# Expert weights in pieces of 16 KB per partition, and the second-last expert's scatter in four PSUM banks

## The chip, the cores and the metric

The kernel runs on one core of one Trainium2 chip. The metric is the device time of one execution in microseconds (us), as the median of three runs. All tensors are fp32.

## What is computed

One layer over 256 latent tokens of width 1024, with 256 context tokens ahead of them. Two mixers (a bidirectional state-space scan and a gated DeltaNet) read the same normalised input; their gated sum goes through an output projection `w_out`. Then comes a mixture of 32 experts, 4 of them per token, and a last RMSNorm. The part that fills most of the time is the mixture:

```python
for e in range(N_EXPERTS):                       # 32
    gu = t @ w_gate_up[e] + b_gate_up[e]         # 1024 -> 2048
    gate, up = gu[:, :D_EXPERT], gu[:, D_EXPERT:]
    gate = jnp.minimum(gate, 7.0); up = jnp.clip(up, -7.0, 7.0)
    act = (up + 1.0) * gate * jax.nn.sigmoid(gate * 1.702)
    out = out + combine[:, e:e + 1] * (act @ w_down[e] + b_down[e])
```

An expert has 8 MB of `w_gate_up` and 4 MB of `w_down`; all 32 have 384 MB (402.7 million bytes), and each byte is read once from HBM.

## The kernel before

**Front** (to about 500 us): modulation, input projection, the two mixers, the branch projections, `merge` (L1307: gates times branches, `w_out`, residual, second norm) and the router. Its large intermediates live in 15 registers of 8 KB per partition (`r`, tags such as XC, R2, H0, PA) and five load buffers (`ld`).

**Experts.** `moe` (L1435) takes one expert after the other. For each, `gather` (L1567) picks up to 64 of its tokens with one-hot matmuls and transposes them to `xT`; `Expert.gu` multiplies by gate-up, one *unit* of 1 MB (128 rows of 2048) after the other, 8 units; `swiglu` (L1686) makes `ut` on VectorE and ScalarE; `down` (L1702) transposes `ut` on PE (`ident,ut`) to `aT` and takes the 4 units of `w_down`; `weigh` (L1721) makes `od` on VectorE, its rounded part `odh` on ScalarE and the rest `odl`; `scatter` (L1733) multiplies these with the one-hot `ST` into PSUM banks and VectorE adds them to `x1` (`x<-x,ps`). A unit is 8 matmuls in the profile, 4 in the order of the program.

**The weights' stream.** 12 units per expert are read in the order in which PE wants them: four gate-up units of the next expert, four of w_down, the other four gate-up units. `wtile` (L1405) takes the places of a ring in turn, `wload` (L1412) issues the load from SP:

```python
WREG = ("K", "XL", "XC", "R2", "U", "H0", "H1", "V", "Q", "R3", "GA") + ("ld",) * 5 + ("PA", "s1", "PB")
NPRE = 10
```

That is 19 places of 1 MB. 18 of them take a unit by one DMA with 8 KB in one piece per partition, "s1" by two DMAs with 4 KB pieces. In `merge` the first load is issued, then the four loads of `w_out` (`wo`), then ten more units; the rest as places come free. SP executes its instructions in the order of the program, so one that waits for a place holds back all behind it. The other engines' order is made by a scheduler from the program. The last expert takes its w_down units in the order 0, 2, 1, 3, and `swiglu` and `down` in two parts.

Of the kernel before, what the change touches and what calls it, by code (L numbers as in the profile page):

```python
# [7 lines left out]
F32 = mybir.dt.float32  # L8
# [8 lines left out]
D = 1024  # L17
EPS = 1e-6
NH = 4
NE = 32  # L20
# [3 lines left out]
def dram(ap, off, dims):  # L24
    return bass.AP(tensor=ap.tensor, offset=ap.offset + off, ap=dims)


class Kern:
# [3 lines left out]
    def build(self):  # L32
        with ExitStack() as es:
            tc = self.tc
            self.con = es.enter_context(tc.tile_pool(name="con", bufs=1))
            self.dr = es.enter_context(tc.tile_pool(name="dr", bufs=1, space=DRAM))
            self.ps = es.enter_context(tc.tile_pool(name="ps", bufs=2, space=PSUM))
            self.consts()
            self.wk = es.enter_context(tc.tile_pool(name="wk", bufs=1))
            with tc.manual_schedule(engines={mybir.EngineType.SP}):  # L40
                self.front()
                self.moe()
# [6 lines left out]
    def w(self, shape, name, tag=None, dt=F32):  # L49
# [7 lines left out]
        assert n <= size, (name, n)  # L57
        return self.wk.tile(list(shape), dt, name=name, tag=tag, bufs=bufs)

    def r(self, reg, name, dt=F32):  # L60

        assert reg in self.REGS
        return self.wk.tile([128, 2048], dt, name=name, tag="r" + reg, bufs=1)

    LD = 5

    def ld(self, name, dt=F32):

# [1311 lines left out]
        self.tt(self.lc, self.lc, p[:, :NE], OP.add)  # L1380


    WREG = ("K", "XL", "XC", "R2", "U", "H0", "H1", "V", "Q", "R3", "GA") + ("ld",) * 5 + ("PA", "s1", "PB")
    NPRE = 10
    HPOOL = [3]
    WOUT = [[0, [0, 1, 2, 3, 4, 5, 6, 7]], [1, [0, 1, 2, 3, 4, 5, 6, 7]]]
    BBP = 0
# [2 lines left out]
    DOWN, DOWN_LAST = (0, 1, 2, 3), (0, 2, 1, 3)  # L1390

    def moe_stream(self):
        I = self.I
        self.nw, self.wq = 0, []
        gu = lambda e, j: dram(I["w_gate_up"], (e * D + j * 128) * 2048, [[2048, 128], [1, 2048]])

        dn = lambda e, f: dram(I["w_down"], (e * D + 512 * (f // 2) + 2 * (f % 2)) * D, [[4 * D, 128], [1, 2 * D]])
        src = [gu(0, j) for j in range(8)]
        n = self.AHEAD
        for e in range(NE):  # L1400
            a = [gu(e + 1, j) for j in range(8)] if e + 1 < NE else []
            src += a[:n] + [dn(e, f) for f in (self.DOWN if a else self.DOWN_LAST)] + a[n:]
        self.wsrc = iter(src)

    def wtile(self):  # L1405
        rg = self.WREG[self.nw % len(self.WREG)]
        self.nw += 1
        if rg == "s1":
            return [self.w([128, D], "w", rg) for _ in range(2)]
        return [self.ld("w") if rg == "ld" else self.r(rg, "w")]  # L1410

    def wload(self, src):  # L1412

        w = self.wtile()
        if len(w) == 1:
            if self.nw == 12 * NE:
                for f in range(2):
                    self.nc.sync.dma_start(w[0][:, f * D:f * D + D], src[:, f * D:f * D + D])
            else:
                self.nc.sync.dma_start(w[0] if len(src.shape) == 2 else w[0].rearrange("p (f c) -> p f c", f=2), src)  # L1420
            return lambda i: w[0][:, 512 * i:512 * i + 512]
        for h in range(2):
            self.nc.sync.dma_start(w[h], src[:, 1024 * h:1024 * h + 1024] if len(src.shape) == 2 else src[:, h])
        return lambda i: w[i // 2][:, 512 * (i % 2):512 * (i % 2) + 512]

    def moe_load(self):
        self.wq.append(self.wload(next(self.wsrc)))

    def moe_weights(self):
        if not self.wq:  # L1430
# [4 lines left out]
    def moe(self):  # L1435
        tc, nc, I = self.tc, self.nc, self.I
# [72 lines left out]
        def expert(e):  # L1509

            keep = None
            if e == NE - 1:
                left = (12 * NE - 1 - self.WREG.index("GA")) % len(self.WREG)
                while self.nw < 12 * NE - left:
                    self.moe_load()
                keep = self.r("GA", "keep")
                self.nf = self.r("R3", "nf")
# [12 lines left out]
        for e in range(NE - 1):  # L1530
            cur.gu(6)
            nxt = expert(e + 1)
            cur.gu(8)
            cur.swiglu()
            nxt.gu(self.AHEAD)
            cur.down(self.DOWN)
            if e == NE - 2:

                cur.weigh()
                nxt.gu(8)  # L1540
                with tc.issue_after(self.last.ins):
                    nxt.swiglu(2)
                    cur.scatter()
            else:
                nxt.gu(self.AHEAD + 1)
                cur.weigh()
                cur.scatter()
            cur = nxt
# [17 lines left out]

    def gather(self, x, pos, cw, io64, keep=None, first=False):  # L1567

        nc = self.nc
        oh = self.w([128, 2, 2, CAP], "oh", "c2")  # L1570
        for t in range(2):
            self.nc.vector.tensor_scalar(oh[:, t], io64[:, None, :].to_broadcast([128, 2, CAP]), pos(t), None,
                                         op0=OP.is_equal)
        xT = self.w([128, 8, CAP], "xT", "p5")
        if first:

            x.xT = xT
            for js in self.FIRST:
                p = self.pt("o").rearrange("p (j s) -> p j s", s=CAP)
                for j in js:  # L1580
                    for t in range(2):
                        self.mm(p[:, j], self.h2[:, t, 128 * j:128 * j + 128], oh[:, t, 0], start=(t == 0), stop=(t == 1))
                x.gu(js[0])
                self.act(xT[:, js[0]:js[-1] + 1], p[:, js[0]:js[-1] + 1], AF.Copy)
        else:

            p = self.pt("o")
            for t in range(2):
                for dh in range(2):
                    self.mm(p[64 * dh:64 * dh + 64], oh[:, t, 0], self.h2[:, t, 512 * dh:512 * dh + 512],  # L1590
                            start=(t == 0), stop=(t == 1))
            xg = self.w([128, 512], "xg", "g5")
            self.act(xg, p, AF.Copy)
            p = self.pt("o")
            for q in range(4):
                self.tr(p[:, 128 * q:128 * q + 128], xg[:, 128 * q:128 * q + 128], self.ident)
            self.act(xT.rearrange("p (d q) s -> p q d s", d=2), p.rearrange("p (q d s) -> p q d s", q=4, d=2), AF.Copy)
        p = self.pt("o")
        for t in range(2):
            o2 = oh[:, t].rearrange("p d s -> p (d s)")  # L1600
            self.tr(p[:, 128 * t:128 * t + 128], o2, self.ident)
# [12 lines left out]
    def overflow(self, pos, cmb, cnt, io64):  # L1614
# [1 line left out]
        tc, nc, I = self.tc, self.nc, self.I  # L1616
        V = nc.vector
        assert not self.wq
        self.WREG = [r for r in self.WREG if r not in ("GA", "R3")]
# [7 lines left out]
        with tc.If(most > CAP):  # L1627
# [10 lines left out]
            with tc.For_i(0, NE, 1) as e:  # L1638
# [3 lines left out]
                for b in range(1, 256 // CAP):  # L1642
                    with tc.If(ce > CAP * b):
# [7 lines left out]
                        wg = I["w_gate_up"][0, bass.ds(e, 1)].rearrange("o (j p) f -> (o p) j f", p=128)  # L1651
                        wd = I["w_down"][0, bass.ds(e, 1)].rearrange("o (h p r) d -> (o p) h r d", p=128, r=4)
                        x = Expert(self, lambda j: self.wload(wg[:, j]), lambda f: self.wload(wd[:, f // 2, 2 * (f % 2):2 * (f % 2) + 2]),
                                   lambda i: (row[:, 128 * i:128 * i + 128], brow), (row[:2, :128], drow))
                        self.gather(x, lambda t: pe[:, t:t + 1], lambda t: pe[:, 2 + t:3 + t], io64)
                        x.gu(8)
# [6 lines left out]
class Expert:  # L1663
# [66 lines left out]
        k.act(oh, od, AF.Copy)  # L1730
        k.tt(ol, od, oh.bitcast(F32), OP.subtract)

    def scatter(self):  # L1733
        k = self.k
        for t in (1, 0):
            ps = [k.pt("s"), k.pt("s")]
            for o in self.od:
                for dh, r in enumerate(self.HALF):
                    k.mm(ps[dh], self.ST[r, 128 * t:128 * t + 128], o[r], start=(o is self.od[0]), stop=(o is self.od[-1]))
# [49 lines left out]
```

## Time and profile before

| | us |
|---|---|
| median of three runs (1449.15, 1453.27, 1454.15) | 1453.27 |
| the profiled execution's own time | 1453.78 |
| its span | 1452.1 |
| PE (TensorE matmuls) busy | 1338.0 (92%) |
| DVE (VectorE) busy | 559.1 (39%) |
| ACT (ScalarE) busy | 255.4 (18%) |
| POOL (GpSimd) busy | 179.1 (12%) |
| DMA traffic of the core | 473.06 MB, mean 326 GB/s |

Busy time is that of one execution; PE's ends are modelled, so a busy PE isn't PE at its peak. PEld is PE's load of the stationary operand, which overlaps its matmuls. A bracket such as [1.57 <-ACT odh L97] says how long the engine stood idle ahead of an instruction and what ended it.

### The profile page before, as it was taken

To read this page: it belongs to the slowest core of one execution; us is meant where nothing else is said; L and a number is where in the kernel's file an instruction comes from. 1 tells how busy PE (TensorE), PEld (TensorE's weight loads), DVE (VectorE), ACT (ScalarE), POOL (GpSimd) and SP (SyncE) were. 2 spreads that over 40 slices of the span, in tenths; PEclk is the share of its full clock that TensorE was granted. 3 is DMA by queue.
4 is the path that set the end of the run, shared out by engine and by line. 5 is a ranking of instruction groups with operands and counts; after the bars stand their busy time and mean duration, and the time that the engine had idled before them with its cause. 6 is when DMAs were issued, how large, how long until landed. Compare 5 with 4: busy or idle time off the path is not lost. (4 is left out here: it accounts for less than half of the span.)

```text
span 1452.1 us, 18531 instructions
## 1 busy us (share of the span) xinstructions
PE 1338.0 (92%) x7469; PEld 600.9 (41%) x7469; DVE 559.1 (39%) x1083; ACT 255.4 (18%) x568; POOL 179.1 (12%) x299
## 2 busy tenths in 40 slices
PE   4799784999999899999999999999999999999985
PEld 1244362768787533333333333333333333333321
DVE  4977977664254403222322322232222222222213
ACT  3224321524301111011110110111011101111001
POOL 1921875111000100000000000000000000000000
PEclk9799896999999899999999999999999999999998
DMA  9464236711638899999999999999999999999994
GB/s 341 193 139 146 88 77 178 223 59 59 197 123 329 281 356 416 419 419 420 419 418 419 420 418 419 419 420 418 419 420 419 418 420 419 419 419 419 419 420 188
DMA packets 93275, 473.06 MB, mean 326 GB/s; under 512 B 24912, under 2 KB 29160, under 8 KB 41344
## 3 DMA queue, kind: packets, MB, share of 16 engines
q1 hardware_dynamic: 73216, 461.08, 79.4%
q10 hardware_dynamic: 19968, 10.73, 3.5%
q8 instruction: 61, 1.00, 0.3%
q14 instruction: 30, 0.25, 0.1%
HBM read 466.52 MB, written 3.16 MB: 323 GB/s over the span
## 5 line engine op out<-in xcount | busy, mean ns | idle before, releaser
L79 PE MATMUL ps<-w,xT 128*64 128x512 f32 x2048 | 485.7, 601 | 9.0 <-DMA w<-in_w_gate_up_dram 8.8
L79 PEld LDWEIGHTS ps<-w,xT 128*64 128x64 f32 x2048 | 137.6, 137 | 272.6 <-issue 241.8
L79 PE MATMUL ps<-w,aT 128*64 128x512 f32 x1024 | 233.1, 597 | 11.4 <-DMA w<-in_w_down_dram 11.1
L1725 DVE SCALAR_TENSOR_TENSOR od<-ps,cs,gt 128x512 f32<-128x512 f32 x31 | 23.3, 750 | 468.7 <-PE ps L79 468.7
L79 PEld LDWEIGHTS ps<-w,aT 128*64 128x64 f32 x1024 | 71.6, 137 | 165.5 <-issue 126.4
L94 DVE TENSOR_TENSOR x<-x,ps 128x512 f32<-128x512 f32 x128 | 84.1, 684 | 66.4 <-PE ps L79 66.4
L1506 POOL CAST selsd<-biad 128x128 fp32r<-128x128 f32 x32 | 9.4, 294 | 703.5 <-PE ps L79 703.5
L97 ACT ACTIVATE odh<-od 128x512 fp32r<-128x512 f32 x31 | 19.5, 629 | 427.0 <-DVE od L1725 427.0
L79 PE MATMUL ps<-h,win 128*128 128x512 f32 x192 | 91.3, 616 | 0.0
L79 PE MATMUL ps<-hx,wsp 128*128 128x256 f32 (+1 forms) x384 | 81.8, 360 | 0.0
L79 PEld LDWEIGHTS ps<-hx,wsp 128*128 128x128 f32 x384 | 62.9, 198 | 20.1 <-issue 9.8
L79 PE MATMUL ps<-h,oh 128*64 128x512 f32 x248 | 63.0, 604 | 0.0
L79 PEld LDWEIGHTS ps<-h,win 128*128 128x128 f32 x192 | 35.0, 195 | 47.6 <-issue 45.8
L97 ACT ACTIVATE sgm<-gt 128x512 f32<-128x512 f32 (+1 forms) x33 | 20.3, 618 | 163.6 <-DVE gt L1696 163.6
L79 PE MATMUL ps<-wm,sc 128*32 128x512 f32 x192 | 29.3, 699 | 20.2 <-DMA wm<-in_w_mod_dram 20.2
L97 ACT ACTIVATE aT<-ps 128x512 f32<-128x512 f32 (+1 forms) x33 | 19.3, 584 | 141.9 <-PE ps L83 141.9
L1696 DVE TENSOR_SCALAR gt<-ps 128x512 f32<-128x512 f32 (+1 forms) x33 | 22.2, 675 | 57.1 <-PE ps L79 57.1
L94 DVE TENSOR_TENSOR wsp<-win,wsp 128x512 fp32r<-128x512 f32 x48 | 32.0, 701 | 23.8 <-ACT wsp L97 23.5
L685 DVE SCALAR_TENSOR_TENSOR cacc<-raw,col_gdn_conv,cacc 128x512 f32<-128x512 f32 (+1 forms) x48 | 36.3, 756 | 5.5 <-ACT cacc L97 5.3
L1506 POOL CAST selsg<-biad 128x256 fp32r<-128x256 f32 x32 | 13.7, 427 | 190.7 <-PE ps L79 184.5
L97 ACT ACTIVATE wsp<-win 128x512 fp32r<-128x512 f32 x48 | 27.5, 624 | 49.2 <-PE ps L79 27.0
L79 PE MATMUL ps<-bias,selsg 128*128 128x512 f32 x64 | 28.6, 472 | 7.1 <-DVE ut L1698 6.6
(367 smaller groups left out, 1465.9 us busy)
## 6 DMA issues: line engine op xcount, KB each, us to landing
w<-in_w_gate_up_dram SPq DMA_DIRECT2D x242, 1024.0 KB
w<-in_w_down_dram SPq DMA_DIRECT2D x121, 1024.0 KB
wm<-in_w_mod_dram SPq DMA_DIRECT2D x24, 1024.0 KB
win<-in_w_in_dram SPq DMA_DIRECT2D x18, 1024.0 KB
w<-in_w_gate_up_dram SPq DMA_DIRECT2D x28, 512.0 KB
w<-in_w_down_dram SPq DMA_DIRECT2D x14, 512.0 KB
wo<-in_w_out_dram SPq DMA_DIRECT2D x4, 1024.0 KB
wa<-in_w_branch_a_dram SPq DMA_DIRECT2D x4, 512.0 KB
```

The source lines that it names most:

```text
L79: self.last = self.nc.tensor.matmul(out, lhsT, rhs, start=start, stop=stop, **kw)
L94: (eng or self.nc.vector).tensor_tensor(out, a, b, op=op)
L97: self.nc.scalar.activation(out, in_, func, **kw)
L685: nc.vector.scalar_tensor_tensor(acc[:, rows], rt[:, rows, k:k + 64], sc, acc[:, rows], op0=OP.mult, op1=OP.add)
L1506: nc.gpsimd.tensor_copy(v.rearrange("p (n s) -> p n s", s=CAP), dup[:, x:x + n, None].to_broadcast([128, n, CAP]))
L1696: V.tensor_scalar(g, z0, 7.0, None, op0=OP.min)
L1725: V.scalar_tensor_tensor(od, self.pd, self.cs, k.gt2, op0=OP.mult, op1=OP.mult)
```

## The change

Twelve registers are joined to six pairs of 16 KB per partition (`PAIRS`: pa = XC and R2, pb = XL and U, pc = H0 and H1, pd = V and Q, pe = R3 and GA, pf = PA and PB), and the front uses their halves. The ring now has nine places of 2 MB. Six are the pairs: each takes two units by one DMA of 2 MB, 16 KB in one piece per partition (gate-up rows 256 j + 2 p and the next; w_down's rows 4 p to 4 p + 3 of one half). The other three are made of "ld" buffers and K and take two DMAs of 8 KB pieces. "s1" is in the ring no more, so it holds 18 MB. The first place of the ring is pa. The last two places of the stream (the last expert's w_down) are loaded in 8 KB pieces, and the very last unit in two halves. Since gate-up rows stand in other partitions, `gather` reads every second column for `xT`. `keep` and the final norm's gain share the tile pe. The second-last expert's `scatter` takes the four PSUM banks s, o, p, g, where it took two of s in turn.

```diff
+    PAIRS = dict(pa=("XC", "R2"), pb=("XL", "U"), pc=("H0", "H1"), pd=("V", "Q"), pe=("R3", "GA"), pf=("PA", "PB"))
+    def both(self, tag, name):
+        return self.wk.tile([128, 4096], F32, name=name, tag=tag, bufs=1)
+    def part(self, tag, half, dt):
+        if tag not in self.pairs:
+            self.pairs[tag] = self.both(tag, "t" + tag)
+        v = self.pairs[tag][:, 2048 * half:2048 * half + 2048]
+        return v if dt is F32 else v.bitcast(dt)
...
-    WREG = ("K", "XL", "XC", "R2", "U", "H0", "H1", "V", "Q", "R3", "GA") + ("ld",) * 5 + ("PA", "s1", "PB")
-    NPRE = 10
+    WREG = ("pa", "pb", "pc", "pe", "pd", "ld", "ld", "k", "pf")
+    NPRE = 4
...
-        gu = lambda e, j: dram(I["w_gate_up"], (e * D + j * 128) * 2048, [[2048, 128], [1, 2048]])
-        dn = lambda e, f: dram(I["w_down"], (e * D + 512 * (f // 2) + 2 * (f % 2)) * D, [[4 * D, 128], [1, 2 * D]])
+        gu = lambda e, j: dram(I["w_gate_up"], (e * D + 256 * j) * 2048, [[4096, 128], [1, 4096]])
+        dn = lambda e, h: dram(I["w_down"], (e * D + 512 * h) * D, [[4 * D, 128], [1, 4 * D]])
...
+        l = dn(NE - 1, 0), dn(NE - 1, 1)
+        src[-2:] = [tuple(x[:, 2048 * i:2048 * i + 2048] for x in l) for i in range(2)]
...
-        if rg == "s1":
-            return [self.w([128, D], "w", rg) for _ in range(2)]
-        return [self.ld("w") if rg == "ld" else self.r(rg, "w")]
+        if rg in ("ld", "k"):
+            return [self.ld("w") if rg == "ld" else self.r("K", "w"), self.ld("w")], None
+        w = self.both(rg, "w")
+        return [w[:, :2048], w[:, 2048:]], w
...
+        (w, whole), dma = self.wtile(), self.nc.sync.dma_start
+        if whole is None and not isinstance(src, tuple):
+            src = src[:, :2048], src[:, 2048:]
+        if isinstance(src, tuple):
+            for i in range(2):
+                n = 2 if (self.nw, i) == (6 * NE, 1) else 1
+                for f in range(n):
+                    c = slice(2048 * f // n, 2048 * (f + 1) // n)
+                    dma(w[i][:, c], src[i][:, c])
+        else:
+            dma(whole, src)
+        return [lambda i, x=x: x[:, 512 * i:512 * i + 512] for x in w]
...
-                    cur.scatter()
+                    cur.scatter("sopg")
...
-                        self.mm(p[:, j], self.h2[:, t, 128 * j:128 * j + 128], oh[:, t, 0], start=(t == 0), stop=(t == 1))
+                        self.mm(p[:, j], self.h2[:, t, 256 * (j // 2) + j % 2:256 * (j // 2) + 256:2], oh[:, t, 0],
+                                start=(t == 0), stop=(t == 1))
...
-                self.tr(p[:, 128 * q:128 * q + 128], xg[:, 128 * q:128 * q + 128], self.ident)
+                self.tr(p[:, 128 * q:128 * q + 128], xg[:, 256 * (q // 2) + q % 2:256 * (q // 2) + 256:2], self.ident)
...
-    def scatter(self):
+    def scatter(self, banks="ssss"):
...
-            ps = [k.pt("s"), k.pt("s")]
+            ps = [k.pt(x) for x in banks[2 - 2 * t:4 - 2 * t]]
```

SP, where the stream starts (`wb` is `w_branch_b`, `tpe` the pair pe that now holds it, `wo_…` are the four loads of `w_out`). Before:

```order
46 L1291 DMA wb<-in_w_branch_b_dram 128x1024 x4
47 L1420 DMA w<-in_w_gate_up_dram 128x2048
48 L1317 DMA wo_3670<-in_w_out_dram 128x2x1024
49 L1317 DMA wo_3672<-in_w_out_dram 128x2x1024
50 L1317 DMA wo_3674<-in_w_out_dram 128x2x1024
51 L1317 DMA wo_3676<-in_w_out_dram 128x2x1024
52 L1420 DMA w<-in_w_gate_up_dram 128x2048 x11
53 L1420 DMA w<-in_w_down_dram 128x2048 x4
```

and with the change:

```order
49 L1307 DMA tpe<-in_w_branch_b_dram 128x1024 x4
50 L1445 DMA w<-in_w_gate_up_dram 128x4096
51 L1333 DMA wo_3631<-in_w_out_dram 128x2x1024
52 L1333 DMA wo_3633<-in_w_out_dram 128x2x1024
53 L1333 DMA wo_3635<-in_w_out_dram 128x2x1024
54 L1333 DMA wo_3637<-in_w_out_dram 128x2x1024
55 L1445 DMA w<-in_w_gate_up_dram 128x4096 x4
56 L1443 DMA w<-in_w_gate_up_dram 128x2048 x2
57 L1443 DMA w<-in_w_down_dram 128x2048 x4
```

The load ahead of the four of `w_out` went to K and now goes to pa; the loads behind them are of 2 MB.

PE, in the middle of the experts, from the transposes of `ut` on (`ident,ut`), to the next expert's units. Before:

```order
980 L83 MATMUL ps<-ident,ut_6224 128x128 x4
981 L79 MATMUL ps<-h_3722,oh 64x512 x4
982 L79 MATMUL ps<-w,xT 64x512 x12
983 L79 MATMUL ps<-w,aT 64x512 x16
984 L79 MATMUL ps<-w,xT 64x512 x4
985 L79 MATMUL ps<-odh,ST 128x512 x2
986 L83 MATMUL ps<-ident,xg 128x128 x4
```

and with the change:

```order
898 L99 MATMUL ps<-ident,ut_5624 128x128 x4
899 L95 MATMUL ps<-h_3671,oh 64x512 x4
900 L95 MATMUL ps<-w,xT 64x512 x8
901 L95 MATMUL ps<-w,aT 64x512 x16
902 L95 MATMUL ps<-odh,ST 128x512 x2
903 L99 MATMUL ps<-ident,xg 128x128 x4
904 L99 MATMUL ps<-ident,oh 128x128 x2
905 L95 MATMUL ps<-small,oh 128x1 x2
```

The unit that stood between the down projection (`w,aT`) and the scatter (`odh,ST`) went ahead of the transposes. Before, one of the experts has `odh,ST` right behind `w,aT`; with the change 15 of 30 have.

PE at the end: the second-last expert's scatter and the last expert's down projection. Before:

```order
1281 L79 MATMUL ps<-w,xT 64x512 x16
1282 L79 MATMUL ps<-odh,ST 128x512 x2
1283 L79 MATMUL ps<-odl,ST 128x512 x2
1284 L79 MATMUL ps<-odh,ST 128x512
1285 L79 MATMUL ps<-odl,ST 128x512
1286 L79 MATMUL ps<-odh,ST 128x512
1287 L79 MATMUL ps<-odl,ST 128x512
1288 L83 MATMUL ps<-ident,ut_8537 128x128 x2
1289 L79 MATMUL ps<-biad,selsd 128x512
1290 L83 MATMUL ps<-ident,ut_8537 128x128 x2
1291 L79 MATMUL ps<-w,aT 64x512 x16
```

and with the change:

```order
1244 L95 MATMUL ps<-w,xT 64x512 x16
1245 L95 MATMUL ps<-odh,ST 128x512 x2
1246 L95 MATMUL ps<-odl,ST 128x512 x2
1247 L95 MATMUL ps<-odh,ST 128x512 x2
1248 L95 MATMUL ps<-odl,ST 128x512 x2
1249 L95 MATMUL ps<-biad,selsd 128x512
1250 L99 MATMUL ps<-ident,ut_8202 128x128 x2
1251 L95 MATMUL ps<-w,aT 64x512 x8
1252 L99 MATMUL ps<-ident,ut_8202 128x128 x2
1253 L95 MATMUL ps<-w,aT 64x512 x8
```

The second half of the scatter goes in pairs, and the last two transposes stand between the two halves of the down projection.

## Rows read from the trace of the kernel before

**Rows 1.** Page, the span in 40 slices (36.3 us each): GB/s.

```profile
GB/s 341 193 139 146 88 77 178 223 59 59 197 123 329 281 356 416 419 419 420 419 418 419 420 418 419 419 420 418 419 420 419 418 420 419 419 419 419 419 420 188
```

**Rows 2.** Busy time in stretches; columns: stretch, length, PE, PEld, DVE, ACT, POOL, PEclk, DMA share, GB/s.

```profile
600.00:700.00 100.00, 100.00 (x456) 36.17 (x452) 28.86 (x52) 12.40 (x27) 2.72 (x8) 1.00 1.01 419
...
1000.00:1100.00 100.00, 96.51 (x442) 33.30 (x440) 27.25 (x48) 11.28 (x23) 2.78 (x8) 1.00 1.01 419
```

**Rows 3.** Timeline of PE, two experts before the engine has caught up with the DMAs.

```profile
734.35 4.03 PE L79 MATMUL ps<-w,aT 128*64 128x512 f32 x18
...
762.49 4.03 PE L79 MATMUL ps<-w,aT 128*64 128x512 f32 x18
```

**Rows 4.** Waits, 1050 to 1420 us; columns: waiting engine, releaser: us, times, longest.

```profile
PE ps L79 <- DMA w<-in_w_down_dram: 11.1, 20, 1.0
...
PE ps L79 <- DMA w<-in_w_gate_up_dram: 7.3, 13, 0.6
```

**Rows 5.** DMA traffic, 1040 to 1070 us: packets, MB, share of 16 engines.

```profile
DMA packets 1728, 12.59 MB, mean 420 GB/s; under 512 B 192, under 2 KB 192, under 8 KB 192
...
q1 hardware_dynamic: 1727, 12.58, 101.0%
```

**Rows 6.** DMA traffic, 1300 to 1340 us.

```profile
DMA packets 2439, 16.72 MB, mean 418 GB/s; under 512 B 271, under 2 KB 271, under 8 KB 527
...
q1 hardware_dynamic: 2437, 16.70, 100.9%
```

**Rows 7.** DMA traffic, 600 to 1400 us, the queue of instruction fetches.

```profile
q8 instruction: 28, 0.46, 0.2%
```

**Rows 8.** Timeline of SP around the start of the stream.

```profile
383.81 0.53 SPq L1420 DMA_DIRECT2D w<-in_w_gate_up_dram  x1
384.44 35.86 SPq L1317 DMA_DIRECT2D wo<-in_w_out_dram  x4
434.87 30.76 SPq L1420 DMA_DIRECT2D w<-in_w_gate_up_dram  x11
```

**Rows 9.** The last readers of the tile vb in XC and R2.

```profile
L94 DVE TENSOR_TENSOR vn<-ps,vb x14: 672/689/695, 386.8 to 440.7; 64x512 f32<-64x512 f32 x14
```

**Rows 10.** Timeline of PE around the output projection.

```profile
450.15 7.03 PE L79 MATMUL ps<-wo,gs 128*128 128x512 f32 x16
...
464.16 20.77 PE L79 MATMUL ps<-wo,gs 128*128 128x512 f32 x48
```

**Rows 11.** Busy time in 5-us stretches where the stream fills up (columns as rows 2).

```profile
440.00:445.00 5.00, 5.00 (x51) 4.66 (x51) 2.22 (x5) 1.47 (x8) 0.58 (x2) 1.00 0.73 263
...
540.00:545.00 5.00, 5.00 (x26) 1.85 (x24) 0.00 (x0) 0.00 (x0) 0.00 (x0) 1.00 0.66 224
545.00:550.00 5.00, 5.00 (x27) 2.28 (x24) 2.75 (x5) 1.11 (x2) 0.00 (x0) 1.00 1.02 428
```

**Rows 12.** Timeline, the one expert whose scatter follows its down projection directly.

```profile
994.09 0.75 DVE L1725 SCALAR_TENSOR_TENSOR od<-ps,cs,gt 128x512 f32<-128x512 f32 x1 [15.14 <-PE ps L79]
994.94 0.63 ACT L97 ACTIVATE odh<-od 128x512 fp32r<-128x512 f32 x1 [14.08 <-DVE od L1725]
...
995.62 0.50 PE L79 MATMUL ps<-odh,ST 64*128 64x512 f32 x2 [1.57 <-ACT odh L97]
```

**Rows 13.** Timeline of the tail: last loads, second-last scatter, last expert.

```profile
1414.43 0.20 PEld L79 LDWEIGHTS ps<-w,xT 128*64 128x64 f32 x4 [1.44 <-DMA w<-in_w_gate_up_dram]
...
1416.93 0.20 PEld L79 LDWEIGHTS ps<-w,xT 128*64 128x64 f32 x4 [1.44 <-DMA w<-in_w_gate_up_dram]
1416.93 3.65 PE L79 MATMUL ps<-w,xT 128*64 128x512 f32 x16 [0.56 <-DMA w<-in_w_gate_up_dram]
...
1419.46 0.23 PEld L79 LDWEIGHTS ps<-w,xT 128*64 128x64 f32 x4 [0.62 <-DMA w<-in_w_gate_up_dram]
...
1422.07 1.94 PE L79 MATMUL ps<-w,xT 128*64 128x512 f32 x8 [1.48 <-DMA w<-in_w_gate_up_dram]
...
1425.79 0.50 PE L79 MATMUL ps<-odh,ST 64*128 64x512 f32 x1 [1.13 <-DVE x L94]
```

More of the change, by code (lines that the diff above doesn't have):

```diff
@@ L38, in build @@
             self.consts()
+            self.pairs = {}
             self.wk = es.enter_context(tc.tile_pool(name="wk", bufs=1))
@@ L58, in w @@
         return self.wk.tile(list(shape), dt, name=name, tag=tag, bufs=bufs)
+    PAIRS = dict(pa=("XC", "R2"), pb=("XL", "U"), pc=("H0", "H1"), pd=("V", "Q"), pe=("R3", "GA"), pf=("PA", "PB"))
+    LD = 5
+    def both(self, tag, name):
[5 more added lines that the diff above has]
+        return v if dt is F32 else v.bitcast(dt)
     def r(self, reg, name, dt=F32):
         assert reg in self.REGS
+        for tag, rs in self.PAIRS.items():
+            if reg in rs:
+                return self.part(tag, rs.index(reg), dt)
         return self.wk.tile([128, 2048], dt, name=name, tag="r" + reg, bufs=1)
-    LD = 5
     def ld(self, name, dt=F32):
@@ L1394, in moe_stream @@
         self.nw, self.wq = 0, []
-        gu = lambda e, j: dram(I["w_gate_up"], (e * D + j * 128) * 2048, [[2048, 128], [1, 2048]])
-        dn = lambda e, f: dram(I["w_down"], (e * D + 512 * (f // 2) + 2 * (f % 2)) * D, [[4 * D, 128], [1, 2 * D]])
-        src = [gu(0, j) for j in range(8)]
-        n = self.AHEAD
+        gu = lambda e, j: dram(I["w_gate_up"], (e * D + 256 * j) * 2048, [[4096, 128], [1, 4096]])
+        dn = lambda e, h: dram(I["w_down"], (e * D + 512 * h) * D, [[4 * D, 128], [1, 4 * D]])
+        src = [gu(0, j) for j in range(4)]
+        n = self.AHEAD // 2
         for e in range(NE):
-            a = [gu(e + 1, j) for j in range(8)] if e + 1 < NE else []
-            src += a[:n] + [dn(e, f) for f in (self.DOWN if a else self.DOWN_LAST)] + a[n:]
+            a = [gu(e + 1, j) for j in range(4)] if e + 1 < NE else []
+            src += a[:n] + [dn(e, h) for h in range(2)] + a[n:]
+        l = dn(NE - 1, 0), dn(NE - 1, 1)
+        src[-2:] = [tuple(x[:, 2048 * i:2048 * i + 2048] for x in l) for i in range(2)]
         self.wsrc = iter(src)
@@ L1407, in wtile @@
         self.nw += 1
-        if rg == "s1":
-            return [self.w([128, D], "w", rg) for _ in range(2)]
-        return [self.ld("w") if rg == "ld" else self.r(rg, "w")]
+        if rg in ("ld", "k"):
+            return [self.ld("w") if rg == "ld" else self.r("K", "w"), self.ld("w")], None
+        w = self.both(rg, "w")
+        return [w[:, :2048], w[:, 2048:]], w
     def wload(self, src):
[L1414 to L1424, printed above, removed]
+        (w, whole), dma = self.wtile(), self.nc.sync.dma_start
[10 more added lines that the diff above has]
+        return [lambda i, x=x: x[:, 512 * i:512 * i + 512] for x in w]
     def moe_load(self):
-        self.wq.append(self.wload(next(self.wsrc)))
+        self.wq += self.wload(next(self.wsrc))
     def moe_weights(self):
@@ L1512, in expert @@
             if e == NE - 1:
-                left = (12 * NE - 1 - self.WREG.index("GA")) % len(self.WREG)
-                while self.nw < 12 * NE - left:
+                left = (6 * NE - 1 - self.WREG.index("pe")) % len(self.WREG)
+                while self.nw < 6 * NE - left:
                     self.moe_load()
-                keep = self.r("GA", "keep")
-                self.nf = self.r("R3", "nf")
+                keep = self.both("pe", "keep")
+                self.nf = keep[:, 2048:]
                 nc.scalar.dma_start(self.nf[:, :D], dram(I["norm_f"], 0, [[0, 128], [1, D]]))
@@ L1618, in overflow @@
         assert not self.wq
-        self.WREG = [r for r in self.WREG if r not in ("GA", "R3")]
+        self.WREG = [r for r in self.WREG if r != "pe"]
         ci = self.con.tile([1, NE], I32, name="ci")
@@ L1650, in overflow, with nxt @@
                         nc.sync.dma_start(drow, I["b_down"][0, bass.ds(e, 1)].rearrange("o (q c) -> (o q) c", q=2))
-                        wg = I["w_gate_up"][0, bass.ds(e, 1)].rearrange("o (j p) f -> (o p) j f", p=128)
-                        wd = I["w_down"][0, bass.ds(e, 1)].rearrange("o (h p r) d -> (o p) h r d", p=128, r=4)
-                        x = Expert(self, lambda j: self.wload(wg[:, j]), lambda f: self.wload(wd[:, f // 2, 2 * (f % 2):2 * (f % 2) + 2]),
+                        wg = I["w_gate_up"][0, bass.ds(e, 1)].rearrange("o (j p r) f -> (o p) j (r f)", p=128, r=2)
+                        wd = I["w_down"][0, bass.ds(e, 1)].rearrange("o (h p r) d -> (o p) h (r d)", p=128, r=4)
+                        src = iter([wg[:, j] for j in range(4)] + [wd[:, h] for h in range(2)])
+                        def nxt():
+                            if not self.wq:
+                                self.wq += self.wload(next(src))
+                            return self.wq.pop(0)
+                        x = Expert(self, lambda j: nxt(), lambda f: nxt(),
                                    lambda i: (row[:, 128 * i:128 * i + 128], brow), (row[:2, :128], drow))
```

## The prediction

> **What bounds the kernel now.** I read the page's slices first, then the busy time in stretches, then who waits for what in the experts, then the two ends of the stream. The rate of the DMAs is flat at 418 to 420 GB/s from the 17th slice, about 580 us, to the last but one [rows 1]. In a stretch early in it PE is busy throughout at full clock, later it is not: 100.00 of 100 us from 600 on, 96.51 from 1000 on, and the DMA share is 1.01 in both [rows 2]. So there are two limits close to each other. An expert costs PE 28.14 us where nothing makes it wait: its down projections start at 734.35 and 762.49 [rows 3]. It costs the DMAs 30.0 us: 12.58 MB, an expert's 12 units, in a stretch of 30 us at 101.0% [rows 5]. PE starts behind a full ring and gains 30.0 - 28.14 = 1.86 us per expert. From about 990 us it has caught up and waits: PE's rows for w_down and w_gate_up show 33 waits for a landing after 1050 us, 18.4 us together [rows 4]. The last gate-up unit lands at 1422.07 [rows 13]. From 990 to there PE could lose (1422 - 990) / 30.0 x 1.86 = 26.8 us before it became the limit. This cover is what the sum turns on.
>
> The time of this kernel is thus: when the stream gets to full rate, then 875 us of full rate, then some 30 us from the last gate-up landing to the end of the span (1452.1).
>
> **1. The start: w_out behind a load that must wait.** Before, the load ahead of the four of w_out is issued at 383.81, since K is free, and w_out follows from 384.44 [rows 8]. Now it goes to pa, which holds vb in one half, and vb is read on VectorE up to 440.7 plus 0.69 [rows 9]. SP waits for that, and behind it wait the four loads of w_out and the whole stream; before, the stream's next loads went from 434.87 [rows 8]. PE wants the first of w_out at 450.15 [rows 10]. To then 3 MB must land from 441: at the 263 GB/s of the stretch from 440 on [rows 11] that takes 3.15 / 0.263 = 12 us, to 453; at full rate 7.5 us, to 449. So PE loses nothing to 4 us; I take the slow price, the one measured in that stretch, less a little: **+2.6**. The next matmuls on w_out are only at 464.16 [rows 10], by when two more MB have landed at either rate. The stream comes after it: places come free when PE has used them, so what PE loses here the stream loses too.
>
> **2. The ring.** It shrinks from 19 MB to 18, and a refill of a pair waits for the second unit in it. That counts while the stream waits for places: in the 5 us from 540 on it moves 224 GB/s, from 545 on 428 [rows 11]. Eight more matmuls on a landed unit add 3.65 - 1.94 = 1.71 us [rows 13]; one unit less of ring and one unit's wait are 2 x 1.71, **+3.4** (bounds 0, if requests on their way cover it, and 5).
>
> **3. Packets.** In a stretch of 30 us the 16 engines were taken for 1.010 x 16 x 30 = 484.8 us by 1535 packets of 8 KB and 192 completions of a few bytes [rows 5], 315 ns each with the completions left out. In another, of 40 us, there are 1910 of 8 KB, 256 of 4 KB (527 under 8 KB less 271 small) and 271 small; 1.009 x 16 x 40 = 645.8 us less 1910 x 0.315 and less the small ones leaves 165 ns for one of 4 KB [rows 6]. Two of 4 KB cost 15 ns more than one of 8. If 16 KB follow that line, a packet takes 615 ns, and a 2 MB load, with 8 packets and a completion fewer on each engine, saves 0.13 us. The landings show less. Whole units land 2.50 us apart (1414.43, 1416.93), the unit in two 512 KB loads has landed 2.53 us after that, at 1419.46 [rows 13]; those 8 packets and one completion more cost 0.03 us. I take 0.04, near the landings, since PE waits for these. It applies to some 113 loads of 2 MB from 545 us on (192 pairs, two thirds of them in pairs' places, less the first ring and the last two) and to 19 units that go through s1 no more: 132 x 0.04 = **-5.3** (bounds -4.0 and -17.2). A negative saving would need packets that cost more than the line; the only ones of 16 KB in this trace, 28 instruction fetches, 0.46 MB in 0.2% of 16 x 800 us, took about 0.9 us each [rows 7], another kind of transfer.
>
> By the Trainium skill, "DMA: Bandwidth & Descriptors", section "Bandwidth", loads of 16 MB were measured at 425 GB/s and those of 1 MB at 341; this trace has 419 with 1 MB, so that table's step isn't seen here, and an estimate from 419 to 425 would be -12 us. The same section's ceiling of 435 GB/s would allow -32 us, and no row here shows it.
>
> **4. The scatter behind the down projection.** In the before's order a unit of the next expert covers the time in which VectorE and ScalarE make od and odh. In one expert it does not: od 0.75 at 994.09, odh 0.63 at 994.94, and PE stands still 1.57 us [rows 12]. The change puts 15 of 30 there: 15 x 1.57 = 23.6 us of PE (bounds 0, where a landing is awaited anyway, and 15 x 2.2, if the transposes of the gathered rows behind it wait for their copy as well, 0.6). With the 2.6 of part 1 that is 26.2, against a cover of 26.8. So it is free, by 0.6 us. This is the tightest place of the forecast: if part 3 shortens the stream, the cover shrinks with it, to 26.8 - 5.3 + 3.4 = 24.9 at the end, 1.3 too little; that eats 1.3 of the packets' gain.
>
> **5. The tail.** The last gate-up units land as one pair, so PE does two units behind the landing and not one: **+1.7** [rows 13]. The four banks take away PE's wait of 1.13 us for VectorE's addition, and a smaller one behind it [rows 13], but the transposes behind still want ut from the same VectorE: 0, bounds -1.3 and +0.5. The last w_down units are due later than they land in either order: 0.
>
> **6. The rest.** The gather's columns with a stride of 2: the transposes of ut read with a stride of 4 already and run without a wait of their own; 0. Fewer DMA instructions on SP: SP mostly waits; 0.
>
> **Sum.** 2.6 + 3.4 - 5.3 + 1.3 + 1.7 = +3.7 on the profiled 1453.78. I take off 1.2, because parts 1 and 2 share their time: what PE loses at 450 gives the loads 2.6 us longer to fill the first ring. That leaves **+2.5, 1456.3**; the profiled run is 0.5 above the median of the runs, so against 1453.27 I say **1456.0**.
>
> **Rivals.**
> - *The packets win.* The full 0.13 us per load, -17.2, the stalls of part 4 mostly fall where PE awaits a landing anyway: -17.2 + 2.6 + 3.4 + 1.7 = -9.5, **1444**. For: the packet times are a straight line. Against: landings show a quarter of it, and before PE catches up each stall counts in full, so PE would have to lose under 0.8 us in each of the 15.
> - *PE becomes the limit* (slower). Each of the 15 costs the upper 2.2 us: 33 + 4 - 26.8 = +10, **1463**. It decides from the point where a place loses more than (26.8 - 2.6 + 3.7) / 15 = 1.86 us; the one measured is at 1.57 with what follows not counted. Then no gain of the DMAs counts.
> - *16 KB packets are off the line*, like the fetches: 0.3 us x 8 per load x 113 = +270 us, **1720**. Nothing but that row speaks for it [rows 7].
> - *The pieces change nothing and the front's delay is hidden*: the stream is at its ceiling; +1.7, 1455, inside the forecast.
>
> **How the numbers follow.** About 0.5%, 7.3 us, is what a measurement of this kernel can tell from no change, so the bounds are 1446.0 and 1460.5. The forecast and the last rival have 0.52, the packets 0.22, PE as the limit 0.24, packets off the line 0.02. The range takes in most of the first two rivals: 1444 to 1464; the forecast's own is 1448 to 1460. Faster 0.22, same 0.52, slower 0.26.
>
> **What would show it.** In the changed kernel's DMA queue packets of 16 KB at 0.615 us, and a rate above 419 GB/s from 600 on (424 by the packets, 421 by the landings). The first matmul on w_out at 452 or 453 with a wait for its load. PE waiting for odh some 15 times, 1.57 us each. After 1050 us fewer waits of PE for w than before. From the last gate-up landing to the end 1.7 us more. I am wrong if the rate hardly rises or falls, if PE waits for the stream as long as before (then part 4 is too dear), or if the start shows no wait.

## The result, and the profile after

The changed kernel takes 1462.84 us as the median of four runs (1462.09 to 1463.6), the kernel before 1452.87 beside it. The ratio is 1.0073, 95% interval [1.0053, 1.0092]: slower by 10 us, or 0.7%, and clear of the noise. The profiled execution took 1462.09, its span is 1460.4.

The stream did what it was built for. The page's row of GB/s in 40 slices of 36.5 us, the counterpart of [rows 1], has 422 to 427 where 418 to 420 stood:

```profile
GB/s 339 201 136 144 82 74 182 221 59 70 136 28 348 361 324 407 419 425 422 425 427 423 423 424 424 425 427 423 424 423 425 426 424 424 424 423 425 426 420 95
```

The DMA traffic from 600 to 1400 us (packets, MB, share of 16 engines), which answers to [rows 5, 7]:

```profile
DMA packets 31010, 339.31 MB, mean 424 GB/s; under 512 B 3444, under 2 KB 3444, under 8 KB 3444
...
q1 hardware_dynamic: 30973, 338.78, 100.6%
```

339.31 MB went in 800 us, in 30973 packets of the stream's queue, of which 3444 are completions. The 338.78 MB in 27529 packets of 16 or 8 KB make 13826 of the former; with 315 ns for one of 8 KB, and the completions taken off as in the prediction, 617 ns are left for one of 16, as the straight line of the prediction said (615).

But from its first unit on PE has become the limit. These are PE's waits from its first unit to the last gate-up unit (engine, line, releaser: us in total, times, longest), the four largest:

```profile
PE ps L95 <- ACT odh L113: 23.6, 15, 1.6
PE ps L95 <- DVE x L110: 5.9, 10, 0.9
PE ps L99 <- DVE ut L110: 3.1, 1, 3.1
PE ps L95 <- DVE ut L1729: 1.0, 3, 0.4
```

No wait for a weight is left, where [rows 4] had 33 of them with 18.4 us. PE also loses clock. Busy time in stretches (columns as rows 2):

```profile
600.00:700.00 100.00, 98.42 (x448) 36.59 (x444) 22.93 (x41) 11.27 (x24) 2.38 (x7) 1.00 1.01 424
900.00:1000.00 100.00, 93.97 (x420) 34.06 (x418) 25.04 (x44) 10.76 (x22) 2.68 (x8) 0.97 1.01 424
980.00:1000.00 20.00, 17.23 (x67) 6.43 (x65) 6.64 (x12) 2.79 (x6) 0.43 (x2) 0.83 1.00 421
1000.00:1100.00 100.00, 96.39 (x445) 35.16 (x443) 22.42 (x40) 10.69 (x22) 2.51 (x7) 0.98 1.01 424
```

Against [rows 2], the granted clock is 0.97 and 0.98 in hundreds of microseconds that had 1.00; in the stretch from 980 on it is 0.83. Last, the start. PE's timeline (start, duration, engine, line, operation) around w_out, at the first unit and at the last, for [rows 10, 13]:

```profile
455.99 5.27 PE L95 MATMUL ps<-wo,tpf 128*128 128x512 f32 x8 [4.68 <-DMA wo<-in_w_out_dram]
...
508.99 3.68 PE L95 MATMUL ps<-w,xT 128*64 128x512 f32 x8
...
1426.43 7.04 PE L95 MATMUL ps<-w,xT 128*64 128x512 f32 x32
```

and the first unit in the kernel before:

```profile
502.00 3.68 PE L79 MATMUL ps<-w,xT 128*64 128x512 f32 x8
```

The 10 us can be followed in three stretches of the profiled executions. *Start*: to the first unit of the first expert, 502.0 before, 508.99 now: +7.0. *Stream*: from there to the end of the last gate-up unit, 922.0 before, 924.5 now: +2.5, though the DMAs were some 10 us faster. *Tail*: from there to the end of the span, 28.1 before, 26.9 now: -1.2. Their sum is the 8.3 us between the spans.

So nearly all of the difference lies ahead of the first unit; behind it the changed kernel takes 951.4 us to the end of its span, the kernel before 950.1. A late start is passed on in full: experiments 8 and 12 below keep the front of the kernel before, their first units start at 497.0 and 498.9, and from there it is again 922.1 and 921.9 us to the end of the last unit.

The 7.0 us of the start have three parts. 4.68 are the wait for w_out, and 1.1 more lie between w_out's first matmul and the first unit. The other 1.2 are that PE comes to w_out late: at 451.31 (455.99 less the wait), where it came at 450.15. The profiled pair shows this part too small, since the changed kernel's run was 1.6 us ahead at a matmul that stands early in both fronts:

```profile
110.82 1.08 PE L79 MATMUL ps<-W,le 64*64 64x512 f32 x4
```

```profile
109.20 1.07 PE L95 MATMUL ps<-W,le 64*64 64x512 f32 x4
```

From there to the point where PE wants w_out it is 336.1 to 339.3 us in the three profiled kernels with the front of before (before, experiments 8 and 12), and 338.5 to 344.2 in the eleven with the changed front: 337.5 and 342.1 on average. So the front on joined registers runs some 4.6 us longer. Which of its steps does it was not followed further.

### The profile page after: what moved, and what is told of

Read it like the earlier page. It is cut to its first block, busy times and chain, and to the rows that moved or that the text cites. A ratio compares the mean times of both kernels' runs of the same rounds, so it can differ in the third digit from the quotient of the medians.

```text
span 1460.4 us, 18231 instructions
## 1 busy us (share of the span) xinstructions
PE 1339.4 (92%) x7469; PEld 617.2 (42%) x7469; DVE 555.2 (38%) x1083; ACT 254.2 (17%) x568; POOL 181.7 (12%) x299
## 5 line engine op out<-in xcount | busy, mean ns | idle before, releaser
L95 PEld LDWEIGHTS ps<-w,xT 128*64 128x64 f32 x2048 | 143.3, 139 | 274.1 <-issue 269.8
L95 PE MATMUL ps<-w,aT 128*64 128x512 f32 x1024 | 228.0, 592 | 1.0 <-ACT aT L113 1.0
L95 PE MATMUL ps<-tpc,win 128*128 128x512 f32 x192 | 91.7, 618 | 0.0
L95 PE MATMUL ps<-hx,wsp 128*128 128x512 f32 (+1 forms) x384 | 79.3, 353 | 0.0
L95 PE MATMUL ps<-odh,ST 64*128 64x512 f32 x124 | 34.9, 494 | 26.9 <-ACT odh L113 23.6
L95 PEld LDWEIGHTS ps<-tpc,win 128*128 128x128 f32 x192 | 35.0, 194 | 47.0 <-issue 46.0
L95 PEld LDWEIGHTS ps<-odh,ST 64*128 64x128 f32 x124 | 13.1, 183 | 78.4 <-ACT odh L113 41.7
L110 DVE TENSOR_TENSOR wsp<-win,wsp 128x512 fp32r<-128x512 f32 x48 | 34.0, 735 | 21.9 <-ACT wsp L113 21.7
```

The source lines that it names most:

```text
L95: self.last = self.nc.tensor.matmul(out, lhsT, rhs, start=start, stop=stop, **kw)
L110: (eng or self.nc.vector).tensor_tensor(out, a, b, op=op)
```

## The experiments

Three theories stood against each other: the late start counts in full; PE's stalls behind the down projections have used up its cover, so that it is the limit; or the stream itself (its larger pieces, its smaller ring) holds PE up. Twelve runs, all on the order and the loads.

**1. w_out first.** The four loads of w_out go ahead of the stream's first load.

```diff
         self.moe_stream()
-        self.moe_load()
         wo = []
...
-        for _ in range(self.NPRE):
+        for _ in range(self.NPRE + 1):
```

> The changed kernel with the four loads of w_out ahead of the first load of the stream. Theory (PE is the limit, and what it loses at the start it never gets back): PE's wait of 4.68 us for w_out goes, the first expert's first unit starts some 5 us earlier than 508.99, nothing waits for weights behind it, and the time falls by about 5, to 1458. Rival (the stream of 2 MB pieces is the limit, the start is hidden): the start moves and the end doesn't, 1462 to 1463.

Measured: 1462.45, ratio to the kernel before 1.0069 [1.0049, 1.009]: no gain. PE's wait for w_out is gone (its matmuls start at 451.76), yet the first unit starts at 508.42. What came late next is a small load on ScalarE's queue. The timeline of this kernel:

```profile
480.43 1.12 ACTq L1475 DMA_DIRECT2D braw<-in_b_gate_up_dram  x2
...
488.76 0.63 ACT L113 ACTIVATE bias<-braw 128x512 fp32r<-128x512 f32 x1 [6.17 <-DMA braw<-in_b_gate_up_dram]
...
490.26 0.93 PE L95 MATMUL ps<-bias,selsg 128*128 128x512 f32 x2 [2.85 <-DVE bias L110]
```

```profile
508.42 3.22 PE L95 MATMUL ps<-w,xT 128*64 128x512 f32 x8
```

The bias is asked for at 480.43 and there at 488.76, after a wait of ScalarE of 6.17 us (3.12 in the kernel before, where the same load took 5.1 us from 478.82); PE stands 2.85 us for it. In that time the stream's loads keep the DMAs busier than before (busy time from asking to use, the kernel before and then this one):

```profile
478.82:483.89 5.07, 5.07 (x13) 2.22 (x12) 1.52 (x3) 0.72 (x3) 0.63 (x2) 1.00 0.69 225
```

```profile
480.43:488.76 8.33, 6.98 (x23) 3.34 (x21) 1.52 (x3) 0.72 (x2) 0.63 (x2) 1.00 1.00 371
```

That the bias is late for this reason was not tried by itself. From w_out's first matmul to the first unit it is 56.7 us here, 51.9 in the kernel before [rows 10]. The wait is only part of these 4.8 us: behind it the granted clock is 0.56 in the 5 us from 490 on and 0.50 in the next ten, where the kernel before still has 1.00 from 490 to 495. The router's matmuls show it, the kernel before and then this one:

```profile
490.24 1.87 PE L79 MATMUL ps<-wra,x1T 128*128 128x32 f32 x16
```

```profile
497.89 3.46 PE L95 MATMUL ps<-wra,tpf 128*128 128x32 f32 x16
```

In experiment 11, where PE doesn't wait for the bias, w_out's first matmul and the first unit are 52.2 us apart. So the theory of the start fell in this form: the wait for w_out is real, and taking it away alone uncovers another one that costs as much.

**2. The scatter behind a unit**, in the changed kernel:

```diff
                 nxt.gu(self.AHEAD + 1)
                 cur.weigh()
-                cur.scatter()
+                with tc.issue_after(self.last.ins):
+                    cur.scatter()
```

> The changed kernel with each scatter held behind a unit of the next expert, so that no scatter follows its down projection directly. Theory: PE's 15 waits of 1.57 us for odh go, and with them the stretches at half clock behind them (about 10 us); PE then catches up with the stream, waits for weights again, and the stream's 424 GB/s sets the end: 1452 to 1454. Rival 1 (the stalls are hidden behind the stream, only the 7 us of the start count): 1461 to 1463. Rival 2 (the front's delay and the stalls count, but the packets bring nothing): 1460.

**3. Both edits.**

> The two edits together. Theory: the stream saturates about 5 us earlier than in the kernel with the order alone and runs at 424 GB/s: 1446 to 1449, below the kernel before (1452.9). Rival (packets bring nothing): 1453 to 1455.

Measured: 1465.21, 1.0087 [1.0066, 1.0108], and 1464.65, 1.0084 [1.0063, 1.0105]. Neither theory nor rival: the 15 waits for odh are gone, and the time didn't fall (both intervals overlap that of the changed kernel). Two waits took their place. Eight experts now have their transposes of gathered rows right behind the down projection and wait 2.06 us each for the copy (`<-ACT xg`, 16.5 us in all). And there is one long wait near the end. The timeline of the kernel with both edits:

```profile
1398.72 0.69 DVE L1730 SCALAR_TENSOR_TENSOR ut<-ut,gt 128x512 f32<-128x512 f32 x1
...
1411.88 0.33 ACTq L1539 DMA_DIRECT2D keep<-in_norm_f_dram  x1
1412.26 0.38 ACT L113 ACTIVATE keep<-ps 128x256 f32<-128x256 f32 x1 [15.04 <-DMA w<-in_w_gate_up_dram]
...
1412.74 0.16 DVE L110 TENSOR_TENSOR cs<-cs 128x1 f32<-128x1 f32 x1 [13.33 <-ACT cs L113]
1412.81 0.68 DVE L110 TENSOR_TENSOR ut<-ut,sgm 128x512 f32<-128x512 f32 x1
...
1413.64 1.10 PE L99 MATMUL ps<-ident,ut 128*128 128x128 f32 x4 [11.55 <-DVE ut L110]
```

PE waits 11.55 us for ut of the second-last expert. VectorE was at ut at 1398.72; the next step of it stands behind cs in VectorE's order, cs waits for ScalarE's keep, and keep for the load of the final norm's gain ahead of it on that engine (its line 1539; 1540 in the changed kernel), which in turn waits for transfers of the stream. The kernel before has the same wait on ScalarE, but ut was through by then. The changed kernel has it too, 3.10 us at 1413.73.

**4. Both edits, 8 KB pieces** (each pair by two DMAs of 1 MB):

```diff
-            dma(whole, src)
+            for i in range(2):
+                dma(w[i], src[:, 2048 * i:2048 * i + 2048])
```

> As the two edits together, but each pair of the ring is loaded by two DMAs of 1 MB with 8 KB pieces, same ring, same places, same order. Theory (16 KB pieces raise the rate from 419 to 424 GB/s, 10 us over the 875 us of full rate): 419 GB/s again and 1456 to 1458. Rival (the piece's size is worth nothing; the gain is in the ring or the order): within 2 us of the kernel with 16 KB pieces.

Measured: 1479.15, 1.0181 [1.0159, 1.0204], at 419 GB/s. The rate answers as the theory says, the time does not: the same wait is 21.9 us here, so up to 10.3 of the 14.5 us between the two kernels may be its doing.

**5 to 7. The gain of the norm loaded later**, on ScalarE's queue behind the last gate-up unit, with both edits, with both and 8 KB pieces, and with another ring:

```diff
-                nc.scalar.dma_start(self.nf[:, :D], dram(I["norm_f"], 0, [[0, 128], [1, D]]))
...
                 with tc.issue_after(self.last.ins):
+                    nc.scalar.dma_start(self.nf[:, :D], dram(I["norm_f"], 0, [[0, 128], [1, D]]))
                     nxt.swiglu(2)
```

> The two edits together (w_out first, scatter behind a unit), and the load of the final norm's gain, on ScalarE's queue, moved from ahead of the last expert's gather to behind its last gate-up unit. In the kernel without this move PE stands still 11.6 us at the second-last expert's transposes: VectorE's ut is queued behind cs, cs behind ScalarE's keep, keep behind that load, and the load behind an earlier transfer of the stream. Theory (that chain ate what the two edits gave): the wait goes to 1 or 2 us and the time falls to 1449 to 1454. Rival (the weights would have stopped PE there anyway): 1462 to 1465.

> The same with 8 KB pieces in all places (two DMAs of 1 MB per pair). Without the move its wait there is 21.9 us. Theory (pieces set the stream's rate, 419 against 424 GB/s): 1457 to 1461, 7 to 10 us above the kernel with 16 KB pieces. Rival (the 14.5 us between the two kernels without the move came from that wait alone): within 2 us of it.

The third has the scatters behind a unit, and a ring that starts in K and a load buffer, so that the load ahead of w_out goes to a place that is free early:

```diff
-    WREG = ("pa", "pb", "pc", "pe", "pd", "ld", "ld", "k", "pf")
-    NPRE = 4
+    WREG = ("k", "pa", "pb", "pc", "pe", "pd", "ld", "ld", "pf")
+    NPRE = 5
```

> The changed kernel with the ring's first place made of K and a load buffer (free early, so that w_out isn't held back, and one more pair ahead of the stream), the scatters behind a unit, and the norm's gain loaded late. Theory (the start, the stalls and the chain at the end are all that the change lost, and 16 KB pieces gain 10 us): the first unit starts at 502 to 505 and the time is 1443 to 1448, below the kernel before. Rival (the front's order is made anew and the start stays late): 1449 to 1453.

Measured: 1459.46, 1.0042 [1.0028, 1.0056]; 1474.03, 1.0143 [1.0127, 1.016]; 1462.11, 1.0062 [1.0047, 1.0076]. All above what the theory said. ut is free now, but the load was still put ahead of aT on ScalarE, and PE waits 6.4, 14.1 and 10.0 us for aT. The first kernel:

```profile
1405.60 0.33 ACTq L1562 DMA_DIRECT2D keep<-in_norm_f_dram  x1
1406.03 0.60 ACT L113 ACTIVATE aT<-ps 128x512 f32<-128x512 f32 x1 [14.23 <-DMA w<-in_w_down_dram]
...
1406.67 9.13 PE L95 MATMUL ps<-w,aT 128*64 128x512 f32 x32 [6.44 <-ACT aT L113]
```

**8. The stalls alone, in the kernel before.** The scatter goes right behind its down projection in the same 15 experts, and behind a unit in the other 15:

```diff
+                if e in (5, 6, 8, 9, 12, 14, 15, 17, 18, 20, 21, 24, 26, 27, 29):
+                    cur.weigh()
+                    cur.scatter()
+                    with tc.issue_after(cur.first.ins):
+                        nxt.gu(self.AHEAD + 1)
+                else:
                     nxt.gu(self.AHEAD + 1)
                     cur.weigh()
-                    cur.scatter()
+                    with tc.issue_after(self.last.ins):
+                        cur.scatter()
```

(`first` is the first scatter's last matmul of `odh`.)

> The kernel before, with the scatter put right behind its down projection in the same 15 experts as in the changed kernel, and behind a unit in the other 15; nothing else. Theory (each costs PE 1.57 us and in some cases a few us at half clock behind it, 34 us in all against a cover of 27): 1457 to 1461. Rival (24 us of stalls without clock loss, inside the cover): 1452 to 1454.

Measured: 1452.4, 0.9991 [0.998, 1.0002]: nothing, as the rival said. PE's waits from the first unit to the last:

```profile
PE ps L79 <- ACT odh L97: 23.6, 15, 1.6
...
PE ps L79 <- DMA w<-in_w_gate_up_dram: 2.5, 3, 1.4
```

The 23.6 us are all there; PE's waits for weights have gone from 19.9 us to 2.5, and those for ut (6.6 us in 22 waits before) to 3.0. The stalls ate the cover nearly to its end and no further. The stream took 922.1 us from the first unit to the last, as before. The clock stayed at 1.00 in every stretch from 520 to 1400 us.

**9 and 10. The gain loaded from SP**, behind the whole stream, so that nothing waits behind it, with 16 KB and with 8 KB pieces (both with w_out first and the scatters behind a unit):

```diff
         cur.down(self.DOWN_LAST, 2)
+        nc.sync.dma_start(self.nf[:, :D], dram(I["norm_f"], 0, [[0, 128], [1, D]]))
```

> The two edits together (w_out first, scatters behind a unit), and the norm's gain loaded from SP's queue behind the whole stream, so that nothing on ScalarE or VectorE stands behind that load. Theory (the wait on ScalarE's queue only moved from ut, 11.6 us, to aT, 6.4 us, when the load was moved on that queue; the stream itself takes 910 to 912 us from the first unit to the last): PE has no wait above 3 us from the first unit to the last gate-up unit, and the time is 1448 to 1453. Rival (the weights' landings stop PE there anyway): 1457 to 1461.

> The same kernel with 8 KB pieces in all places. Theory (16 KB pieces are worth 419 against 424 GB/s, and PE has to wait for the stream in both): 918 to 921 us from the first unit to the last, 7 to 10 us above the kernel with 16 KB pieces, 1457 to 1462. Rival (without the wait on ScalarE's queue the piece's size makes no difference): within 2 us of it.

Measured: 1457.51, 1.0039 [1.0025, 1.0053], and 1460.7, 1.0065 [1.0045, 1.0086]. The long wait is gone in both; the longest left in the first is 2.97 us, for a weight. The time fell by 7.1 against the kernel with both edits, less than the 12 that the wait had shown, since the weights stop PE a little behind it, as the rival said. From the first unit to the last it is 915.5 with 16 KB pieces and 924.1 with 8 KB, 8.6 apart; of the totals only 3.2 are left, and their intervals overlap, which fits neither theory nor rival. The tail takes 3.2 of the difference back, 29.0 us against 25.8; the rest is not explained (the first units of the two profiled executions start 7 us apart). PE's timeline there, 16 KB first:

```profile
1419.47 8.62 PE L95 MATMUL ps<-w,xT 128*64 128x512 f32 x32 [2.97 <-DMA w<-in_w_gate_up_dram]
...
1432.19 5.35 PE L95 MATMUL ps<-w,aT 128*64 128x512 f32 x16 [0.53 <-ACT aT L113]
```

```profile
1433.84 3.65 PE L95 MATMUL ps<-w,aT 128*64 128x512 f32 x16 [0.53 <-ACT aT L113]
```

The same 16 matmuls take 5.35 us in one and 3.65 in the other: part of them ran at half clock (granted 0.83 from 1430 to 1440 in the first, 1.00 in the second).

**11. All repairs**: the ring that starts in K, the scatters behind a unit, the gain from SP, and the last gate-up pair by two DMAs.

```diff
+        g = src[-3]
+        src[-3] = g[:, :2048], g[:, 2048:]
         self.wsrc = iter(src)
```

> Ring with its first place in K and a load buffer, scatters behind a unit, the norm's gain from SP behind the stream, and the last gate-up pair loaded by two DMAs of 1 MB. Theory (all that the change lost is put back, and the 16 KB pieces' gain is left): 1444 to 1449, below the kernel before (1453). Rival (PE's own work and the late start are the limit): 1450 to 1455.

Measured: 1454.63, 1.0019 [1.0006, 1.0032]: 8 us better than the change, still not better than the kernel before, as the rival said. In the profiled execution, the fastest of the twelve, the stretch from the first unit to the last takes 915.7 us, 6.3 less than before, so most of the packets' gain is there; it is spent ahead of the first unit, which starts at 504.48. Even there PE stands still or slows down: it keeps eight waits of 2.06 us for xg, and the granted clock is 0.97 or 0.98 in four of the hundreds of microseconds from 700 on.

**12. The second part of the change alone**, in the kernel before:

```diff
-                    cur.scatter()
+                    cur.scatter("sopg")
```

(with the banks' names passed to `scatter` as in the change).

> The kernel before with the second part of the change alone: the second-last expert's scatter over four banks. Theory: PE's waits of 1.13 and 0.20 us for VectorE's additions go, the transposes behind wait for ut instead; -1.5 to +0.5, no difference that can be measured, 1451 to 1454. Rival (the four banks free PE for the last down projection): -3, 1450.

Measured: 1453.56, 1.0014 [0.9999, 1.0029]: no difference that can be told. PE's waits of 1.13 and a little for the additions go [rows 13], and a wait of 1.51 us for ut comes in their place (PE's timeline of this kernel; the changed kernel has it too, at 1436.53):

```profile
1421.29 0.40 PE L79 MATMUL ps<-odh,ST 64*128 64x512 f32 x2
...
1421.84 0.50 PE L79 MATMUL ps<-biad,selsd 128*128 128x512 f32 x1
1423.85 0.61 PE L83 MATMUL ps<-ident,ut 128*128 128x128 f32 x2 [1.51 <-DVE ut L94]
```

## Why the prediction was right or wrong

The range held the time: 1462.84 lies near its upper end, 1464. The forecast itself, 1456.0 and no difference that can be told, did not come; what came has the sign of the second rival, PE as the limit, and its signs in the profile: no wait for weights, 15 waits for odh. That its 1463 is nearly to the point is luck: it was 15 times 2.2 us of stalls and 4 of the start against a cover of 26.8; measured were 15 times 1.57, 7.0, and a cover some 10 us smaller.

On the profiled run the forecast was +2.5: the start +1.4 (2.6 - 1.2), the stream -0.6 (3.4 - 5.3 + 1.3), the tail +1.7. Measured are +8.3: +7.0, +2.5 and -1.2. So two steps failed. The start is short by 5.6 us, the largest miss; the stream by 3.1, since its gain was counted though PE could not follow. The tail's 2.9 the other way hide most of the second. (The forecast's last step should give 1455.8 instead of 1456.0, a slip of no weight.)

- **1, the start, mis-sized**: +2.6 for w_out was 4.68, measured, and the upper bound of 4 too low. The first matmul on it was forecast for 452 or 453 and came at 455.99. Experiment 1 shows more: this wait isn't a term that can be taken off, since the bias, late as well, would hold PE next. The longer front, some 4.6 us ahead of w_out, was not in the sum at all, though the change joins twelve of its registers. The first unit was 7.0 us late in the profiled run.
- **2, the ring**: not tested alone. PE never waits for a weight in the changed kernel, so the ring's size set nothing.
- **3, the packets**: mechanism right, size too small. 424 against 419 GB/s over 875 us are 10.3 us where 5.3 were taken (bounds 4.0 and 17.2). By the row of the packet's duration it was nearly exact, 617 against 615 ns. The prediction weighed the Trainium skill, "DMA: Bandwidth & Descriptors", section "Bandwidth", whose 425 GB/s, stated there for loads of 16 MB, gave an estimate of -12 us for the stream: on the rate, the trace agrees, with 424 GB/s in loads of 1 and 2 MB. Experiments 9 and 10 show the gain in the stream, 8.6 us; in the changed kernel it was worth nothing, as PE was the limit.
- **4, the scatter behind the down projection**: 15 x 1.57 = 23.6 us came exactly. That they are free by the cover was right for the kernel before: experiment 8 shows it. **The step that failed** is the sum "26.2, against a cover of 26.8", which counted the stalls alone. Missing were the half clock, about 10 us (the five stretches of 20 us with a clock below 0.95 are short by 0.17, 0.07, 0.09, 0.09 and 0.09 of their 20; four lie behind waits for odh, the last behind the wait for ut), 5.9 us of waits for VectorE's additions, and the 3.10 us for ut. The faster stream also shrank the cover by all of its 10 us: the prediction named this and let it cost 1.3. These terms add up to too much: 42.8 us against a cover of 16.5 would be 26 beyond the DMAs' time, and the stretch from the first unit to the last is some 13 beyond it (924.5 against 922.0 - 10.3). Some 8 of the other 13 were in the kernel before as well: the "28.14 us where nothing makes it wait" hold a wait for ut of 0.30 us each, 6.6 in all and 1.0 now, and it had 2.3 us of other waits for odh and ut. Some 5 us are not accounted for.
- **5, the tail**: +1.7 was -1.2. The last pair had landed before PE came to it, so its landing cost nothing. The four banks: 0, as forecast, and shown alone in experiment 12. What shortened the tail by 1.2 was not tried.
- **6**: the strided reads showed no wait of their own.

What stays open: the cause of the longer front, which no experiment took away, and the exact size of the start, since the same front's first unit starts up to 5 us apart from run to run (497.0 to 502.0 in the three profiled kernels that have it). That the late start and PE's limit make the 10 us between them is read from the traces; no run took both away and came out faster than the kernel before. The chain of keep, cs and ut was not taken out of the changed kernel alone.

## What to carry to other kernels

A faster stream pays only as far as the engine it feeds has time in hand: measure that cover, in the stretch where the two run side by side, before pricing the stream. When a change makes a scheduler lay the program out anew, read the new order for every place where an engine's next instruction needs a result that another has yet to make, small loads on a second queue included; here these places cost more than the DMAs gave. Look at the part ahead of the stream as well: what is late there is late at the end. Taking one late thing away shows the next one behind it, so repair them together and measure the sum.

## What the runs showed of the hardware that was not expected

The clock can fall behind a wait of 1.57 us, and whether it did went with what PE did next. In the changed kernel eight of the 15 waits for odh are followed by the scatter's two matmuls and then by transposes (`ident,xg`), and behind four of these the granted clock went to 0.66 (once) or 0.83 (three times) in the 10 us that follow, the lower of the two levels for part of them; seven are followed by a unit's matmuls (`w,xT`), and none lost clock. In experiment 8 all 15 are followed by a unit and none lost clock. One of the four, in PE's timeline:

```profile
983.78 0.50 PE L95 MATMUL ps<-odh,ST 64*128 64x512 f32 x2 [1.58 <-ACT odh L113]
984.27 0.77 PE L99 MATMUL ps<-ident,xg 128*128 128x128 f32 x4
...
986.77 6.08 PE L95 MATMUL ps<-w,xT 128*64 128x512 f32 x16
```

and one of experiment 8:

```profile
711.02 0.50 PE L79 MATMUL ps<-odh,ST 64*128 64x512 f32 x2 [1.57 <-ACT odh L97]
711.45 1.94 PE L79 MATMUL ps<-w,xT 128*64 128x512 f32 x8
```

Two units took 6.08 us behind the transposes, where two take 3.65 at full clock [rows 13]. A clock event thus cost 1.7 to 3.4 us, as much again as the wait ahead of it or more. The waits for the bias are of the same kind, with small matmuls behind them: 2.85 us in experiment 1, and 1.48 in the third of 5 to 7, with a clock of 0.50 in the 5 us from 490 on. Also new: packets of 16 KB lie on the straight line of those of 4 and 8 KB (165, 315, 617 ns), while the fetches of 16 KB take about 0.9 us [rows 7].
